# Two heads in turns on the two row halves of the array, in a three-layer mixer network on one core

## The chip, the cores and the metric

The kernel runs on 1 core of one Trainium2 chip. The metric is the time of one execution in device microseconds (us); shorter is better. Before the change the median of three runs is 2854.15 us (2843.81 to 2860.08).

## What is computed

One input of 512 tokens by 1024 features goes through a first block and two layers of a second block, all in float32. Cut to the parts that matter here:

```python
# first block: attention heads and a gated delta rule, 8 heads of 64 features, chunks of 64 tokens
a_mat = where(strict, (k_beta @ k.T) * decay, 0)           # per chunk, per head
qk    = where(causal, (q @ k.T) * decay, 0)
# after a triangular solve (u, w), chunk by chunk:
v_new = u - w @ state
o     = (q * exp(g)) @ state + qk @ v_new
state = state * exp(g_last) + k_dec.T @ v_new

# second block, each of two layers: three mixers a, b, c of 4 heads
#   a: heads of 128 features, c: heads of 64 features: a scan with decays by token, forward and backward
#   b: retention, heads of 64 features: scores (k.T q) * table of decays by distance, then times v
merged = sigmoid(gate_a) * (y_a @ w_pa) + sigmoid(gate_b) * (y_b @ w_pb) + sigmoid(gate_c) * (y_c @ w_pc)
x = x + g1 * (merged @ w_out)
# each block ends in a feed forward layer: (silu(h @ w_gate) * (h @ w_up)) @ w_down
```

## The kernel before, in words

Activations lie with features on the 128 partitions and the 512 tokens free. A large product (`proj`, L125) streams a strip of 128 weight columns from memory (`strip`, L104), splits it into two float32r parts on ScalarE and VectorE (`split`, L100), and sums three matmuls for each of up to 8 tiles of the contraction (`mm3`, L119 to L123: high by high, high by low, low by high). These products fill most of TensorE's time and are independent of one another within a stage.

PSUM is used through two tags of one bank a tile: `mm` with three buffers for the large products, `mx` with five for all else (L85 to L89). A buffer of `mx` is given out again only after what was in it has been read by VectorE or ScalarE.

Work is written as chains (delta rule, attention, scans, retention) into which a list of large products (`Dense`, L38) is mixed: `fill(us)` takes products worth about so many microseconds, by fixed costs. A framework then schedules the instructions of each engine by priority and its own cost model; on each engine they run in the order so found, and semaphores make them wait for their operands and buffers.

Many products contract over only 64 partitions, because two heads of 64 features share a tile: head e lies on partitions 64 e to 64 e + 63. Such a product uses one half of the array's rows. They are:

- `delta_pairs(h)` (L722): for each of 8 heads, four products k by k (L733) and four q by k (L734) of 64 rows, 128 columns, 128 tokens, into two tiles `mx`.
- `delta_out(t)` (L860): for each of 4 pairs of heads one tile `mx`. For each head and each tile of 128 tokens, a product of the masked scores (L870, 128 rows, 64 columns: the head's half of the columns), then one or two products with the state (L874, 64 rows and 64 columns: the head's quarter).
- `scan` (L1067): ten levels; s is 0 (the diagonal), then 1, 2, 4 to 256. At each level the two halves of every block of 2 s tokens meet. Mixer c calls it with two heads of 64 rows, mixer a with one head of 128. Up to s = 16 a level is 16 products per head of 32 columns (L1104); s = 32 and 64 go to L1123 (32 and 64 columns), s = 128 to L1135, s = 256 to `mm3` on the tiles `far`. Between levels VectorE multiplies the decays into `R` (L1154) and, up to s = 16, ScalarE copies the keys into `kt` (L1085); scores are written out into S by `split`.
- `retention(h)` (L1303): for each of 4 heads four tiles of scores, each one `mm3` over 64 rows (tile `bqk`, 512 tokens), then a product with the table of decays (L1315) and a `split` into `Sb`.

All four take one head after the other. In the scan, at s = 32 and 64, the loop over blocks b (which choose the columns of the array) is outside the loop over the tiles j of tokens, also in mixer a. In the second block retention of head h + 1 stands between the two halves of the work on head h (`mid`, a merge of 36 matmuls, L1433 to L1440).

Of the kernel before, what the change touches and what calls it, by code (L numbers as in the profile page):

```python
# [34 lines left out]
class Dense:  # L35
# [34 lines left out]
class Net:  # L70
# [78 lines left out]
    def first_pair(self):  # L149
        """the strips read at the start, behind the products that the next tiles of the operand wait for"""  # L150
# [8 lines left out]
    def go_on(self, last):  # L159
        """the next stage of the norm under way, its products after the one given"""  # L160
# [4 lines left out]
    def last_pair(self, ws, act, kn, then, norm):  # L165
        """two strips, one half of the tokens after the other; then(i, ps, sl) takes each, norm(sl) follows a half"""
# [16 lines left out]
    def proj_tok(self, w, act, dst):  # L183
        """tokens on partitions, 256 features free; dst(tt) takes tokens tt and tt + 1"""
# [68 lines left out]
    def setup2(self):  # L253
# [9 lines left out]
        # lower bounds of the second layer's forget gates  # L263
# [19 lines left out]
    def ada(self, li, g, part):  # L283
        """columns 512 g and on of layer li's modulation, a part of the rows"""
# [32 lines left out]
    def ada_sum(self):  # L317
        """a group's sum over the partitions, traced late so that it waits for nothing"""
# [15 lines left out]
    def ada_rows(self, li, g0, g1):  # L334
        """columns g0*1024 .. g1*1024, from rows to features on partitions"""
# [20 lines left out]
    def ada_first(self):  # L356
        """shift and gain of the first norm, some feature tiles at a time"""
# [67 lines left out]
    def stat(self, f, gained=False, sl=slice(0, T)):  # L425
        """running sums of squares, after x's tile f is final"""
# [11 lines left out]
    def rstd(self, hi, lo):  # L438
        """from squares over a head's partitions; 1 / 128 is exact"""
# [9 lines left out]
    # the norm's factors: a column for each tile of 128 tokens  # L449
# [21 lines left out]
    def spread(self, c):  # L471
        """columns to rows, on all partitions"""
# [1133 lines left out]
```

## Time and profile before

| | |
|---|---|
| runs | 2843.81, 2854.15, 2860.08 us, median 2854.15 |
| span of the profiled execution | 2841.0 us, granted TensorE clock 0.994 of full speed |
| TensorE (PE) busy | 2774.7 us, 98% |
| TensorE weight loads (PEld) busy | 2234.6 us, 79% |
| VectorE (DVE) busy | 1721.8 us, 61% |
| ScalarE (ACT) busy | 1172.0 us, 41% |
| DMA | 330.66 MB, mean 116 GB/s |

No time is given for the profiled execution apart from its span, so the span is taken as its own time; the fastest run is 2.8 us longer, the median 13.2 us.

How to read it: a matmul of this trace overlaps the next, so a row's time or an instruction's mean is longer than what it adds to the engine's time; the start of one row to the start of the next row is what the first one costs. A product in float32 stands in the trace as two matmuls (the program's one L870 is x2), one in float32r as one. The shapes read rows*columns of the array, then partitions x elements of the moving operand: `64*128 64x512` is 64 contracted rows, 128 columns, 512 tokens.

### The profile page before, as it was taken

What the parts mean: (1) busy time and instruction counts of PE and PEld (TensorE: products, weight loads), DVE (VectorE), ACT (ScalarE), POOL (GpSimd) and SP (SyncE); (2) the same over time, 40 slices, a digit from 0 to 9 for tenths busy, and PEclk for the clock granted to TensorE, in tenths of its full rate; (3) what the DMA queues carried; (4) which work ended last, traced back from release to release, by engine and by line L of the source; (5) the groups of instructions that cost most, each with busy time, mean ns of one, the idle gap of its engine ahead of it and who ended that gap; (6) DMA issues with size and microseconds to landing.
All of it is one profiled execution on the core that took longest, in us unless ns stands there. A gap on an engine that the chain in (4) does not pass through costs nothing.

```text
span 2841.0 us, 42612 instructions
## 1 busy us (share of the span) xinstructions
PE 2774.7 (98%) x17518; PEld 2234.6 (79%) x17518; DVE 1721.8 (61%) x2690; ACT 1172.0 (41%) x1796; POOL 41.7 (1%) x79
## 2 busy tenths in 40 slices
PE   7999999999999999999999999999999999999998
PEld 4786678878888887787887888877877888888887
DVE  4677646747377767756466563567777665533334
ACT  4643324222255655444343222465454443422223
POOL 0011000000000000100000000000000000000000
PEclk9999999999999999999999999999999999999999
DMA  7454524646232222332446463322223324333332
GB/s 259 126 157 117 156 87 144 228 150 215 84 110 62 68 72 68 101 93 83 133 134 210 153 224 93 103 66 68 68 75 90 99 80 130 89 97 96 92 94 82
DMA packets 471315, 330.66 MB, mean 116 GB/s; under 512 B 15447, under 2 KB 426223, under 8 KB 469584
## 3 DMA queue, kind: packets, MB, share of 16 engines
q1 hardware_dynamic: 468176, 320.51, 37.2%
q0 software_dynamic: 2944, 7.43, 0.9%
q8 instruction: 138, 2.26, 0.3%
q14 instruction: 57, 0.47, 0.1%
HBM read 312.55 MB, written 13.24 MB: 115 GB/s over the span
## 4 chain that ended last, share of the span: by engine, by line
PE 89%; DVE 4%; ACT 3%; DMA 2%; issue 1%; SPq 1%; POOL 0%; ACTq 0%; DVEq 0%; POOLq 0%
PE mm L121 22%; PE mm L122 22%; PE mm L123 22%; PE mx L121 3%; PE mx L122 3%; PE mx L123 3%; PE mm L193 1%; PE mm L195 1%; PE mm L194 1%; PE mx L1104 1%; PE mx L1123 1%; ACT whi L101 1%; PE mx L325 1%; PE mx L940 1%; DVE R L1154 1%
## 5 line engine op out<-in xcount | busy, mean ns | idle before, releaser
L121 PE MATMUL mm<-hh,whi 128*128 128x512 f32 (+1 forms) x2248 | 873.0, 391 | 12.4 <-ACT hh L487 9.0
L122 PE MATMUL mm<-hl,whi 128*128 128x512 f32 (+1 forms) x2248 | 876.9, 391 | 2.5 <-DVE hl L488 1.8
L101 ACT CAST whi<-raw 128x1024 fp32r<-128x1024 f32 (+2 forms) x451 | 438.3, 973 | 1068.6 <-PE mm L122 737.9
L123 PE MATMUL mm<-hh,wlo 128*128 128x512 f32 (+1 forms) x2248 | 874.0, 390 | 0.0
L102 DVE TENSOR_TENSOR wlo<-raw,whi 128x1024 fp32r<-128x1024 f32 (+2 forms) x451 | 507.4, 1126 | 361.5 <-ACT whi L101 350.0
L121 PEld LDWEIGHTS mm<-hh,whi 128*128 128x128 f32 x2248 | 419.6, 188 | 113.6 <-ACT hh L487 12.0
L122 PEld LDWEIGHTS mm<-hl,whi 128*128 128x128 f32 x2248 | 422.6, 188 | 102.5 <-DVE hl L488 6.0
L123 PEld LDWEIGHTS mm<-hh,wlo 128*128 128x128 f32 x2248 | 422.5, 188 | 93.4 <-issue 0.8
L122 PE MATMUL mm<-hid,whi 128*128 128x512 f32 (+1 forms) x564 | 212.7, 377 | 0.0
L121 PE MATMUL mm<-hid,whi 128*128 128x512 f32 (+1 forms) x564 | 212.5, 377 | 0.0
L123 PE MATMUL mm<-hid,wlo 128*128 128x512 f32 (+1 forms) x564 | 212.1, 376 | 0.0
L492 DVE SCALAR_TENSOR_TENSOR x<-mm,mod,x 128x512 f32<-128x512 f32 (+1 forms) x116 | 80.4, 694 | 180.6 <-PE mm L123 180.3
L307 DVE SCALAR_TENSOR_TENSOR acc<-araw,cs,acc 128x512 f32<-128x512 f32 x224 | 167.9, 750 | 17.6 <-DMA araw<-in_w_ada_dram 12.9
L542 DVE TENSOR_TENSOR sg<-mm,sg 128x512 f32<-128x512 f32 x66 | 45.6, 691 | 159.5 <-PE mm L123 158.0
L1154 DVE TENSOR_TENSOR R<-R,tot 128x512 f32<-128x512 f32 x192 | 126.0, 685 | 12.5 <-PE mx L1123 10.9
L193 PE MATMUL mm<-whi,hh 128*128 128x256 f32 x448 | 128.7, 287 | 2.0 <-ACT q_all L663 2.0
L195 PE MATMUL mm<-whi,hl 128*128 128x256 f32 x448 | 128.3, 286 | 0.0
L194 PE MATMUL mm<-wlo,hh 128*128 128x256 f32 x448 | 127.7, 285 | 0.0
L121 PEld LDWEIGHTS mm<-hid,whi 128*128 128x128 f32 x564 | 106.2, 188 | 20.4 <-issue 0.8
L122 PEld LDWEIGHTS mm<-hid,whi 128*128 128x128 f32 x564 | 106.2, 188 | 19.2
L123 PEld LDWEIGHTS mm<-hid,wlo 128*128 128x128 f32 x564 | 106.2, 188 | 19.1
L193 PEld LDWEIGHTS mm<-whi,hh 128*128 128x128 f32 x448 | 85.2, 190 | 4.3 <-ACT q_all L663 2.5
(384 smaller groups left out, 3507.2 us busy)
## 6 DMA issues: line engine op xcount, KB each, us to landing
raw<-in_w_in_dram SPq DMA_DIRECT2D x164, 512.0 KB
araw<-in_w_ada_dram SPq DMA_DIRECT2D x48, 1024.0 KB
raw<-in_w_ffn_in_dram SPq DMA_DIRECT2D x88, 512.0 KB
araw<-in_w_ada_dram SPq DMA_DIRECT2D x64, 256.0 KB
raw<-in_w_ffn_out_dram SPq DMA_DIRECT2D x32, 512.0 KB
raw<-in_w_gate_dram SPq DMA_DIRECT2D x22, 512.0 KB
raw<-in_w_up_dram SPq DMA_DIRECT2D x22, 512.0 KB
raw<-in_w_ada_dram SPq DMA_DIRECT2D x16, 512.0 KB
```

What stands on the lines that cost most here:

```text
L101: self.nc.scalar.copy(out=hi, in_=src)
L102: self.nc.vector.tensor_tensor(out=lo, in0=src, in1=hi.bitcast(F32), op=ALU.subtract)
L121: m(out=ps, lhsT=w[0], rhs=a[0], start=first, stop=False)
L122: m(out=ps, lhsT=w[0], rhs=a[1], start=False, stop=False)
L123: return m(out=ps, lhsT=w[1], rhs=a[0], start=False, stop=last)
L193: m(out=o, lhsT=a[0][:, sl], rhs=hi[:, k % 4], start=k == 0, stop=False)
L194: m(out=o, lhsT=a[0][:, sl], rhs=lo[:, k % 4], start=False, stop=False)
L195: m(out=o, lhsT=a[1][:, sl], rhs=hi[:, k % 4], start=False, stop=k == KT - 1)
L307: nc.vector.scalar_tensor_tensor(out=acc, in0=raw, scalar=cs[:, k:k + 1], in1=acc, op0=ALU.mult, op1=ALU.add)
L492: self.nc.vector.scalar_tensor_tensor(out=self.x(f)[:, sl], in0=ps[:, sl], scalar=g[:, f:f + 1], in1=self.x(f)[:, sl], op0=ALU.mult, op1=A ...
L542: nc.vector.tensor_tensor(out=sg, in0=pu, in1=sg, op=ALU.mult)
L1154: v.tensor_tensor(out=o, in0=o, in1=half(1 - c), op=ALU.mult)
```

## The change

The heads of a pair are taken in turns, so that matmuls that follow each other lie on different row halves: `delta_pairs` and `retention` work on a pair of heads at once, `scan` has its loop over heads innermost (and j outside b at s = 32 and 64), and `mm3s` interleaves the three matmuls of several products. `delta_out` first makes all products with the masked scores, the heads in turns, then all those with the state. All instructions other than matmuls stay the same in kind and number, but for three more loads of ScalarE's tables. `retention` now makes both heads' scores before the first `mid` of the pair. Comments are dropped throughout, so line numbers differ.

```diff
+    def mm3s(self, sets, first, last):
+        for i, (x, y) in enumerate(((0, 0), (0, 1), (1, 0))):
+            for ps, w, a in sets:
+                self.nc.tensor.matmul(out=ps, lhsT=w[x], rhs=a[y], start=first and i == 0, stop=last and i == 2)
...
-        def delta_pairs(h):
-            t, e = h // 2, h % 2
-            r = slice(64 * e, 64 * e + 64)
...
-            pk, pq = self.mx(), self.mx()
-            for tt in range(4):
-                sl = slice(tt * P, tt * P + P)
-                nc.tensor.matmul(out=pk[:, sl], lhsT=k_all[r, t, sl], rhs=k_all[r, t, sl], start=True, stop=True)
-                nc.tensor.matmul(out=pq[:, sl], lhsT=k_all[r, t, sl], rhs=q_all[r, t, sl], start=True, stop=True)
+        def delta_pairs(t):
+            gbs, rows = [], [slice(64 * e, 64 * e + 64) for e in range(2)]
...
+            ps = []
+            for x in (k_all, q_all):
+                ps.append([self.mx() for _ in rows])
+                for tt in range(4):
+                    sl = slice(tt * P, tt * P + P)
+                    for e, r in enumerate(rows):
+                        nc.tensor.matmul(out=ps[-1][e][:, sl], lhsT=k_all[r, t, sl], rhs=x[r, t, sl], start=True, stop=True)
...
-            for e in range(2):
-                h, o = 2 * t + e, slice(64 * e, 64 * e + 64)
-                wv = rv[h // 4]
-                for tt in range(4):
-                    sl = slice(tt * P, tt * P + P)
-                    nc.tensor.matmul(out=ps[o, sl], lhsT=wv[:, tt, h % 4, 0:64], rhs=qkm[h // 4][:, h % 4, sl],
-                                     start=True, stop=False)
-                    for c in range(max(1, 2 * tt), 2 * tt + 2):
-                        sl = slice(64 * c, 64 * c + 64)
-                        nc.tensor.matmul(out=ps[o, sl], lhsT=S[o, c, 64 * t:64 * t + 64], rhs=q_all[o, t, sl],
-                                         start=False, stop=c % 2 == 1)
+            hs = [(2 * t + e, slice(64 * e, 64 * e + 64)) for e in range(2)]
+            for tt in range(4):
+                sl = slice(tt * P, tt * P + P)
+                for h, o in hs:
+                    nc.tensor.matmul(out=ps[o, sl], lhsT=rv[h // 4][:, tt, h % 4, 0:64], rhs=qkm[h // 4][:, h % 4, sl],
+                                     start=tt == 0, stop=False)
+            for c in range(1, 8):
+                sl = slice(64 * c, 64 * c + 64)
+                for h, o in hs:
+                    nc.tensor.matmul(out=ps[o, sl], lhsT=S[o, c, 64 * t:64 * t + 64], rhs=q_all[o, t, sl],
+                                     start=False, stop=c == 7)
...
-                    for b in range(P // s):
-                        o, i = slice(s * b, s * b + s), s * (b ^ 1)
-                        for j in range(4):
-                            nc.tensor.matmul(out=ps4[o, j, i:i + s], lhsT=R[r, 1 + b % 2, j * P + s * b:j * P + s * b + s],
+                for j in range(4):
+                    for b in range(P // s):
+                        o, i = slice(s * b, s * b + s), s * (b ^ 1)
+                        for n, r in heads:
+                            m(out=four(near[n])[o, j, i:i + s], lhsT=R[r, 1 + b % 2, j * P + s * b:j * P + s * b + s],
...
-                            self.mm3(ps[:, j * 256:(j + 1) * 256], [a[r, o:o + P] for a in far[0]],
-                                     [a[r, 256 * (1 - b):256 * (2 - b)] for a in far[1]], True, True)
+                        self.mm3s([(ps[n][:, j * 256:(j + 1) * 256], [a[r, o:o + P] for a in far[0]],
+                                    [a[r, 256 * (1 - b):256 * (2 - b)] for a in far[1]]) for n, r in heads], True, True)
...
-        def retention(h):
+        def retention(t):
...
+            S = [[self.t8("Sb", F32R) for _ in range(2)] for _ in range(2)]
+            rows = [slice(64 * e, 64 * e + 64) for e in range(2)]
             for j in range(4):
-                ps = self.mx()
-                self.mm3(ps, [a[r, j * P:(j + 1) * P] for a in st["bk", t]], [a[r] for a in st["bq", t]], True, True)
...
+                ps = [self.mx() for _ in rows]
+                self.mm3s([(ps[e], [a[r, j * P:(j + 1) * P] for a in st["bk", t]], [a[r] for a in st["bq", t]])
+                           for e, r in enumerate(rows)], True, True)
...
-        S = retention(0)
-        for h in range(4):
-            mid(2 * h)
-            o = self.head_out(self.mix(st["bv"], h, S), V[:, 68 + h:69 + h], st["bg", h], y["b"], h)
-            next(o)
-            if h < 3:
-                S = retention(h + 1)
-            mid(2 * h + 1)
-            next(o)
+        for t in range(2):
+            S = retention(t)
+            for e in range(2):
+                h = 2 * t + e
+                mid(2 * h)
+                o = self.head_out(self.mix(st["bv"], h, S[e]), V[:, 68 + h:69 + h], st["bg", h], y["b"], h)
+                next(o)
+                mid(2 * h + 1)
+                next(o)
```

What the change does to TensorE's order, at two places. The first is the delta output, TensorE, before: the first head of a pair (`mx` the output tile, `qkm` and `rr` scores and values, `q_all` and `S` queries and state).

```order
L870 MATMUL mx<-qkm,rr 64x128
L874 MATMUL mx<-q_all,S 64x64
L870 MATMUL mx<-qkm,rr 64x128
L874 MATMUL mx<-q_all,S 64x64 x2
L870 MATMUL mx<-qkm,rr 64x128
L874 MATMUL mx<-q_all,S 64x64 x2
```

The kinds alternate at every token tile, eight times for a pair of heads. The same place now, two pairs of heads, down to the first large product:

```order
L882 MATMUL mx<-qkm,rr 64x128 x8
L887 MATMUL mx<-q_all,S 64x64 x14
L882 MATMUL mx<-qkm,rr 64x128 x8
L887 MATMUL mx<-q_all,S 64x64 x14
L683 MATMUL mx<-consts,osq 128x2 x4
L123 MATMUL mm<-ya,wlo 128x512
```

Each kind now stands in one row per pair of heads, and the work behind it is in the same order as before.

The second place is retention in the first layer of the second block, TensorE, before: head 0, the first of four tiles `mx` being number 10833 (10245 and 10246 are the high and low parts of queries and keys).

```order
L121 MATMUL mx_10833<-bqk_10245 128x512
L122 MATMUL mx_10833<-bqk_10246,bqk_10245 128x512
L123 MATMUL mx_10833<-bqk_10245,bqk_10246 128x512
L121 MATMUL mx_10841<-bqk_10245 128x512
L122 MATMUL mx_10841<-bqk_10246,bqk_10245 128x512
L123 MATMUL mx_10841<-bqk_10245,bqk_10246 128x512
```

After twelve of these a large product follows, and head 1 comes only after that and the product with v. Now, the first pair of heads (10835 is head 0, 10836 head 1):

```order
L129 MATMUL mx_10835<-bqk_10245 128x512
L129 MATMUL mx_10836<-bqk_10245 128x512
L129 MATMUL mx_10835<-bqk_10246,bqk_10245 128x512
L129 MATMUL mx_10836<-bqk_10246,bqk_10245 128x512
L129 MATMUL mx_10835<-bqk_10245,bqk_10246 128x512
L129 MATMUL mx_10836<-bqk_10245,bqk_10246 128x512
L129 MATMUL mx_10851<-bqk_10245 128x512
L129 MATMUL mx_10852<-bqk_10245 128x512
```

Twenty-four stand in a row, heads in turns. The second pair of heads now, from its second tile of scores on (11197 is head 2, 11198 head 3):

```order
L129 MATMUL mx_11197<-bqk_10245 128x512
L129 MATMUL mx_11197<-bqk_10246,bqk_10245 128x512
L129 MATMUL mx_11197<-bqk_10245,bqk_10246 128x512
L121 MATMUL mm_11251<-hh_6430,whi_11246 128x512
L122 MATMUL mm_11251<-hl_6431,whi_11246 128x512
L129 MATMUL mx_11198<-bqk_10245 128x512
L129 MATMUL mx_11198<-bqk_10246,bqk_10245 128x512
L129 MATMUL mx_11198<-bqk_10245,bqk_10246 128x512
```

Here the scheduler takes the heads one after the other again: of this pair only the six matmuls of the first tile are in turns. The second layer has the same order.

## Rows read from the trace of the kernel before

**Rows 1.** The page: TensorE's busy time, and the chain that ended last by engine.
```profile
PE 2774.7 (98%) x17518; PEld 2234.6 (79%) x17518; DVE 1721.8 (61%) x2690; ACT 1172.0 (41%) x1796; POOL 41.7 (1%) x79
...
PE 89%; DVE 4%; ACT 3%; DMA 2%; issue 1%; SPq 1%; POOL 0%; ACTq 0%; DVEq 0%; POOLq 0%
```

**Rows 2.** Busy time by stage, scans of c: length; busy PE, PEld, DVE, ACT, POOL.
```profile
855.00:970.00 115.00, 111.38 (x1401) 90.76 (x1400) 89.98 (x167) 69.06 (x119) 0.00 (x0) 1.00 0.24 66
```

**Rows 3.** Timeline of TensorE, one pair of heads in delta output: start us, us, instructions.
```profile
394.47 1.09 PE L686 MATMUL mx<-c_ident,hc 128*64 128x128 f32 x16 [0.95 <-DVE hc L460]
395.39 0.38 PE L870 MATMUL mx<-qkm,rr 128*64 128x128 f32 x2
...
400.98 0.83 PE L677 MATMUL mx<-consts,osq 128*128 128x2 f32 x6
```

**Rows 4.** Timeline of TensorE, one step of the delta states.
```profile
359.88 0.68 PE L846 MATMUL mx<-S,m 64*64 64x64 f32 x16
360.50 0.50 PE L121 MATMUL mm<-ya,whi 128*128 128x512 f32 x1
```

**Rows 5.** Timeline of TensorE, delta pairs of heads 0 and 1.
```profile
91.85 0.48 PE L733 MATMUL mx<-k_all 64*128 64x128 f32 x2
...
93.30 0.49 PE L733 MATMUL mx<-k_all 64*128 64x128 f32 x4
93.52 0.49 PE L734 MATMUL mx<-q_all,k_all 64*128 64x128 f32 x4
93.85 0.38 PE L733 MATMUL mx<-k_all 64*128 64x128 f32 x2
...
95.28 0.50 PE L121 MATMUL mm<-hh,whi 128*128 128x512 f32 x1
```

**Rows 6.** Timeline of TensorE, one scan of mixer c: s = 1, 32, 64, 128, 256.
```profile
861.36 0.84 PE L1104 MATMUL mx<-R,kt 64*32 64x32 f32 x64 [2.73 <-ACT kt L1085]
...
882.21 1.51 PE L1123 MATMUL mx<-R 64*32 64x32 f32 x64 [0.52 <-DVE R L1154]
...
885.48 1.54 PE L1123 MATMUL mx<-R 64*64 64x64 f32 x32
...
888.78 1.71 PE L1135 MATMUL mx<-R 64*128 64x128 f32 x16
...
897.14 0.51 PE L121 MATMUL mx<-far 64*128 64x256 f32 x4
...
900.22 0.50 PE L121 MATMUL mx<-S,cvh 128*128 128x512 f32 x1
```

**Rows 7.** Groups by line, 338.2 to 340.4 us, delta transitions: busy us, mean ns.
```profile
L819 PE MATMUL mx<-kdec,rr 64*64 64x64 f32 x64 | 2.1, 225 | 0.0
L820 PE MATMUL mx<-qkm,rr 64*64 64x64 f32 x64 | 2.1, 218 | 0.0
```

**Rows 8.** Timeline of TensorE, one scan of mixer a: s = 1, 32, 64.
```profile
988.04 0.55 PE L1104 MATMUL mx<-R,kt 128*32 128x32 f32 x32
...
1005.86 0.90 PE L1123 MATMUL mx<-R 128*32 128x32 f32 x32
...
1008.31 0.97 PE L1123 MATMUL mx<-R 128*64 128x64 f32 x16
```

**Rows 9.** Timeline of TensorE, retention of head 0, start and end.
```profile
1242.38 0.49 PE L121 MATMUL mx<-bqk 64*128 64x512 f32 x1
1242.72 0.39 PE L122 MATMUL mx<-bqk 64*128 64x512 f32 x1
1242.96 0.39 PE L123 MATMUL mx<-bqk 64*128 64x512 f32 x1
...
1245.35 0.50 PE L121 MATMUL mm<-hh,whi 128*128 128x512 f32 x1
```

**Rows 10.** Busy time by stage: scan of c between s = 64 and 256; behind retention.
```profile
887.10:897.10 10.00, 10.00 (x51) 7.79 (x51) 9.01 (x21) 7.25 (x19) 0.00 (x0) 1.00 0.19 54
1243.40:1249.40 6.00, 6.00 (x26) 4.61 (x25) 6.00 (x9) 2.84 (x5) 0.00 (x0) 1.00 0.36 90
```

More of the change, by code (lines that the diff above doesn't have):

```diff
@@ new lines, in delta_pairs @@
+        def delta_pairs(t):
+            gbs, rows = [], [slice(64 * e, 64 * e + 64) for e in range(2)]
+            for e in range(2):
+                h = 2 * t + e
+                gb = self.t2("gb")
+                nc.sync.dma_start(out=gb, in_=bass.AP(gs.tensor, gs.offset + h * T, [[0, P], [1, T]]))
+                v.tensor_tensor(out=four(gb), in0=four(gb), in1=cap(rt, 16 + h, [[32, 4], [0, P]]), op=ALU.subtract)
+                v.scalar_tensor_tensor(out=four(gb), in0=four(gb), scalar=0.0, in1=mask(dmask), op0=ALU.min, op1=ALU.add)
+                nc.scalar.activation(out=gb, in_=gb, func=AF.Exp)
+                gbs.append(gb)
+            ps = []
[5 more added lines that the diff above has]
+                        nc.tensor.matmul(out=ps[-1][e][:, sl], lhsT=k_all[r, t, sl], rhs=x[r, t, sl], start=True, stop=True)
+            for e in range(2):
+                h = 2 * t + e
+                nt = self.t2("nt")
+                v.tensor_tensor(out=nt, in0=ps[0][e], in1=gbs[e], op=ALU.mult)
+                nc.gpsimd.dma_start(out=nts[4 * h:4 * h + 4].rearrange("t (j i) -> j t i", j=P), in_=four(nt))
+                last = v.tensor_tensor(out=four(noff[h // 4][:, h % 4]), in0=four(nt), in1=mask(off), op=ALU.mult)
+                v.tensor_tensor(out=qkm[h // 4][:, h % 4], in0=ps[1][e], in1=gbs[e], op=ALU.mult)
+            if t == 1:
@@ L975, in mixer1 @@
             delta_tok(t)
-            for e in range(2):
-                delta_pairs(2 * t + e)
+            delta_pairs(t)
             q_decay(t)
@@ L1091, in scan @@
                 yield
-            for n, r in heads:
-                if s <= 16:
-                    if lv % 4 == 0:
+            m = nc.tensor.matmul
+            if s <= 16:
+                if lv % 4 == 0:
+                    for n, r in heads:
                         small[n] = self.mx()
-                    ps = small[n][:, (lv % 4) * P:(lv % 4) * P + P]
-                    for j in range(4):
-                        for b in range(4):
-                            o = j * P + 32 * b
+                pss = {n: small[n][:, (lv % 4) * P:(lv % 4) * P + P] for n, r in heads}
+                for j in range(4):
+                    for b in range(4):
+                        o = j * P + 32 * b
+                        for n, r in heads:
                             if s == 0:
@@ L1115, in scan @@
                             put(n, o, 32 * b, [[T + P, 4], [1, 32]], four(sd[n][o]))
-                elif s <= 64:
-                    if s == 32:
+            elif s <= 64:
+                if s == 32:
+                    for n, r in heads:
                         near[n] = self.mx()
-                    ps4 = four(near[n])
+                for j in range(4):
                     for b in range(P // s):
                         o, i = slice(s * b, s * b + s), s * (b ^ 1)
-                        for j in range(4):
-                            nc.tensor.matmul(out=ps4[o, j, i:i + s], lhsT=R[r, 1 + b % 2, j * P + s * b:j * P + s * b + s],
-                                             rhs=R[r, 3 - 3 * (b % 2), j * P + i:j * P + i + s], start=True, stop=True,
-                                             tile_position=(r.start, s * b))
-                    if s == 64:
+                        for n, r in heads:
+                            m(out=four(near[n])[o, j, i:i + s], lhsT=R[r, 1 + b % 2, j * P + s * b:j * P + s * b + s],
+                              rhs=R[r, 3 - 3 * (b % 2), j * P + i:j * P + i + s], start=True, stop=True,
+                              tile_position=(r.start, s * b))
+                if s == 64:
+                    for n, r in heads:
                         for s2 in (32, 64):
```

71 lines of the change are left out of this document (31 added, 40 removed).

## The prediction

> **What bounds the kernel now.** I read the page's busy times and its chain first, then the busy times by stage, then TensorE's timeline at each of the products that the change touches, and last what VectorE does there.
>
> TensorE is busy 2774.7 us of a span of 2841.0, and 89% of the chain that ended last lies on it [rows 1]. So a matmul that takes less of the array's time shortens the end, provided that the next thing on TensorE is ready. The second half of this sentence is open only in the scans and retention: in the first scans of mixer c TensorE is busy 111.4 of 115 us, but VectorE 90.0 [rows 2], and single levels already start late, by 0.52 us behind VectorE and 2.73 us behind ScalarE [rows 6]. In the delta rule the products stand in queues of large products that need nothing of them.
>
> **How products on parts of the array run, by rows.** Three places in this trace show it. First, column halves: the products L686 (64 columns, halves in turns) take 0.92 us for 16 records from their start to the next row's start [rows 3]. Second, quarters: in the delta states L846 the even head is on rows and columns 0 to 63, the odd one on 64 to 127, in turns and into one tile; 16 records take 0.62 us [rows 4]. And in the delta transitions, where all four quarters come in turns, 128 records of the same size take 2.1 us, 16 ns each [rows 7]. Third, row halves with all 128 columns, which is what most of the change needs: there is no such sequence, but one seam. In delta pairs 32 records take 3.43 us from 91.85 to 95.28, so four take 0.43. At the step from head 0 to head 1, eight records take only 0.55 us, from 93.30 to 93.85, instead of 0.86 [rows 5]. The last product of one head and the first of the next lie on different halves there, so they overlap: the eight cost 0.64 of their serial time. As a seam has a serial product at each side, I take this as the upper bound of a pair's price and 0.5 as the lower one, and work with 0.55.
>
> **The sum, part by part** (a row's start to the next row's start is its cost; where rows of one kind are compared, their own lengths do).
>
> *Delta output*, four pairs of heads. One pair costs 400.98 - 395.39 = 5.59 us [rows 3]: 16 records of L870 and 28 of L874 that change kind sixteen times. Grouped, the 16 records are of L686's shape, in column halves in turns: 0.92 us [rows 3]. The 28 are of L846's: 28/16 of 0.62 = 1.09 us [rows 4]. The sum is 2.0, the gain 3.6 a pair, **14.3 us**. What follows on TensorE, the norm's sums over the pair before, is one round behind and stays covered by the next pair's 2.0 us.
>
> The two heads' state products here write one tile from two row halves. The Trainium skill (TensorEngine Tiling (Array Packing), Restrictions and Gotchas, Gotcha 1) says that different row tiles cannot access the same PSUM bank at the same time. The states L846 do just that and reach 39 ns a record, where 64 by 64 products that mostly stay in one quarter need (1.54 us for 32) 48 [rows 4, 6], so the trace speaks against the rule; by the rule the 28 records would cost 1.35 us instead of 1.09, and the sum would be 1 us smaller.
>
> *Delta pairs*, four: 3.43 us each [rows 5] become 0.55 of that, 1.89: **6.2 us** (4.9 to 6.9 by the two prices). The group now holds four tiles `mx` of five at once instead of two and two; the two transposes ahead of it occupy two, whose last reader is done before the second pair of tiles is asked for, so I charge nothing but cover it with 0.8 us below.
>
> *Scans of c*, four (two layers, two pairs of heads) [rows 6]. s = 32: 64 records in 1.51 us; the same number and size at s = 1, where the column groups come in turns, takes 0.84: 0.67. s = 64: 1.54 us become the transitions' 32 x 16 ns = 0.5 plus a tail of 0.2: 0.84 [rows 6, 7]. s = 128: 1.71 us at 0.55 to 0.6 with the tail: 0.7. s = 256: from 897.14 to 900.22 are 3.08 us with one large product of about 0.25 inside; 0.45 of the other 2.83 goes: 1.27 (1.0 to 1.4). The sum is 3.48 a scan, **13.9 us**. Levels up to s = 16 already cost some 13 ns a record with four column groups; eight tiles instead of four may give up to 0.1 us a level. I count nothing.
>
> *Scans of a*, eight [rows 8]: here only b and j change places, so that column groups come in turns. s = 32: 0.90 becomes the 0.55 of s = 1: 0.35. s = 64: 0.97 becomes the 0.68 of L846, two halves in turns [rows 4]: 0.29. **5.1 us**.
>
> *Retention*, four heads in each of two layers. Twelve products cost 2.97 us from 1242.38 to 1245.35 [rows 9]. The first pair of heads, 5.94, becomes 24 products in turns, at 0.55 3.27 us. But now eight tiles of scores pass through five buffers: VectorE gives a buffer back after an instruction of 0.67 us (nine instructions in the 6.00 us behind the group, without a pause [rows 10]), and its splits stand in between. The sixth to eighth tile wait for the first three, about 0.8 us. That leaves 1.9. Of the second pair of heads the scheduler keeps six products in turns and takes the rest apart: 0.65 gained, and 0.1 lost for each time that TensorE changes between these and large products more often than before (1242.72 - 1242.38 is 0.34, the next step 0.24 [rows 9]): 0.5. **4.8 us** for both layers (2 to 7).
>
> The parts add up to 14.3 + 6.2 + 13.9 + 5.1 + 4.8 = **44.3 us**.
>
> *What comes back.* Between s = 64 and 256 in the scan shown, VectorE is busy 9.0 of 10.0 us, TensorE all of it with large products [rows 10]. The work of VectorE there (decays, 14 pieces of scores to split, a strip) doesn't shrink, and only its start moves. Of the 1.5 us saved at s = 64 and 128 I let 1.2 come back as a wait at s = 256, in one of two scans a layer (the other has more large products in that place): 2.4. In the scans of a 1.2 for all eight, in delta pairs 0.8. Edits without cost: the nt product ahead of qkm in delta pairs moves no work, three more table loads lie on ScalarE, at 41% [rows 1], behind large products. 44.3 - 4.4 = 39.9 us. Against the profiled execution that is 2841.0 to 2801.1, and with the same difference the median of 2854.15, which lies 13.2 above that span, becomes **2814 us**.
>
> **Rivals.**
>
> *Evictions decide in the second block.* If in the scans and in retention VectorE and ScalarE are always the later ones, TensorE's gain there (13.9 + 5.1 + 4.8) returns as waits, and only the delta rule's 19.7 us stay: 2834. For it speaks VectorE at 78% [rows 2] and the levels that start late [rows 6]; against it, that a level's products are part of the chain themselves: VectorE can't update R before they end, so it starts earlier too. The Trainium skill (TensorEngine Tiling (Array Packing), Performance Considerations, PSUM Bottleneck) warns of this: tiling speeds up TensorE, not the reading of PSUM. Chance 0.16.
>
> *Row halves with 128 columns don't run side by side.* Then delta pairs, s = 128, s = 256 and retention (6.2 + 2.8 + 5.1 + 4.8) gain nothing, and some 24 us are left: 2830. The seam speaks against it [rows 5]. Chance 0.07.
>
> *Slower: TensorE stands at full buffers.* It takes its instructions in order, and both heads' tiles are now filled before either is read. If every eviction had to be waited for, retention would hold TensorE for eight times two instructions of 0.67 us, 10.7 less its own 3.3, four times: 30 us; s = 128 and 256, with eight such instructions beyond their products, four times 5: 21; delta pairs, six evictions of 0.67 less 1.9, four times: 8. That is 59 against 44.3, some 15 us slower: 2869. It decides only if over three quarters of these evictions are uncovered. Against it: behind each group stand large products that need no `mx` tile. Chance 0.03.
>
> *The change doesn't do what it says*: the scheduler separates the heads, as it does in half of retention, or what is gained is lost in the placing of large products. About 2852, chance 0.05.
>
> **How the numbers follow.** The forecast has 0.69. A measurement of this kernel can tell about 0.5% from no change, 14.3 us: faster by more than that is below 2839.9. The forecast and nearly all of the first two rivals lie there: 0.88; the same 0.09; slower 0.03. The range: at the low end all bounds at their best and nothing coming back (44.3 + 6, so 2804) and runs that differ by 16 us among themselves, 2797; at the high end both rivals around 2830 to 2834, 2837.
>
> **What would show it.** Right: the rows of delta output at about 2 us a pair; eight records of delta pairs in some 0.47 us; TensorE's busy time about 44 us lower at the same count of records; its waits at `R`, `kt` and `far` up by less than 6 us. Wrong: matmuls of different halves that start one after the other; TensorE waiting at L129 for the products with the table; VectorE without pauses through whole scans while TensorE waits.

## The result and the profile after

The changed kernel takes 2814.27 us (median of 4 runs, 2812.23 to 2818.36) against 2854.11 us of the kernel before in the same series: ratio 0.987, 95% interval 0.985 to 0.989. A second series gave 2816.97 against 2850.55, ratio 0.988 (0.986 to 0.990). It is 1.3% faster, with an interval that lies clear of 1, and where the prediction put it. The page of the profiled execution, span 2810.5 us:

```profile
PE 2743.8 (98%) x17518; PEld 2203.2 (78%) x17518; DVE 1718.7 (61%) x2690; ACT 1173.7 (42%) x1799; POOL 41.7 (1%) x79
```

The count of matmuls is the same, TensorE's busy time is 30.9 us lower [rows 1], the span is 30.5 us shorter. The forecast said 44 and 40; where the difference lies is the question of the runs below. First the places that the prediction named.

TensorE's timeline (start us, us, instructions, idle time before), one pair of heads in delta output: 1.94 us from 382.45 to 384.39, instead of 5.59 [rows 3]; 2.0 was forecast.

```profile
382.45 1.04 PE L882 MATMUL mx<-qkm,rr 128*64 128x128 f32 x16
383.43 1.03 PE L887 MATMUL mx<-q_all,S 64*64 64x64 f32 x28
384.39 1.05 PE L683 MATMUL mx<-consts,osq 128*128 128x2 f32 x8
```

Delta pairs of heads 0 and 1 are 2.28 us, from 88.78 to 91.06, instead of 3.43 [rows 5]. The forecast was 1.89. The second pair of heads, from 111.89, needs only 1.99 us.

```profile
88.78 1.16 PE L744 MATMUL mx<-k_all 64*128 64x128 f32 x16
...
91.06 0.50 PE L121 MATMUL mm<-hh,whi 128*128 128x512 f32 x1
...
111.89 1.16 PE L744 MATMUL mx<-k_all 64*128 64x128 f32 x16
...
113.88 0.50 PE L121 MATMUL mm<-hh,whi 128*128 128x512 f32 x1
```

The difference is a buffer. In the first group the fourth tile must wait until VectorE has read the transposes of v, and that instruction runs into the group:

```profile
89.18 0.68 DVE L726 TENSOR_TENSOR rr<-mx,rt 128x512 f32<-128x512 f32 x1
```

The first products of head 1 with q start 0.23 us behind those of head 0, and the group is 0.29 us longer for it. The third group has the same wait (2.16 us), the fourth doesn't (1.99).

The first scan of c, by the rows' lengths: s = 32 is 0.76 us (1.51 before), s = 64 0.69 (1.54), s = 128 1.16 (1.71) [rows 6]. At s = 256, by starts and with the large product that stands inside, it is 2.43 us from 876.54 to 878.97 instead of 3.08.

```profile
863.57 0.76 PE L1139 MATMUL mx<-R 64*32 64x32 f32 x64 [0.64 <-DVE R L1174]
...
866.08 0.69 PE L1139 MATMUL mx<-R 64*64 64x64 f32 x32
...
868.72 1.16 PE L1153 MATMUL mx<-R 64*128 64x128 f32 x16
...
876.54 0.50 PE L129 MATMUL mx<-far 64*128 64x256 f32 x4
876.97 0.50 PE L121 MATMUL mm<-hh,whi 128*128 128x512 f32 x1
...
878.97 0.49 PE L121 MATMUL mx<-S,cvh 128*128 128x512 f32 x1
```

At s = 256 the gain is 0.65 us in this scan, where 1.27 was forecast. The kernel before shows why:

```profile
897.58 0.50 PE L121 MATMUL mm<-hh,whi 128*128 128x512 f32 x1
898.01 0.38 PE L122 MATMUL mx<-far 64*128 64x256 f32 x1
...
898.83 0.28 PE L123 MATMUL mx<-far 64*128 64x256 f32 x1
898.83 0.38 PE L122 MATMUL mx<-far 64*128 64x256 f32 x1
```

The large product inside costs 0.43 us from its start to the next, not the 0.25 of the prediction, so the other 24 cost 2.65. And these 24 were not all one after the other: the first four, two of each head, take 0.44 us from 897.14 [rows 6], as the four do that are now in turns (0.43), and where head 1 follows head 0 the last products of one and the first of the other start together (898.83). Some ten of the 24 already ran in pairs.

Behind the scan stand the products with its scores S, TensorE, and VectorE's part of writing S out of the tiles `mx`, the changed kernel and then the kernel before:

```profile
879.69 0.50 PE L122 MATMUL mx<-S,cvh 128*128 128x512 f32 x1 [0.23 <-DVE S L102]
...
878.95 1.89 DVE L102 TENSOR_TENSOR S<-mx,S 128x512 fp32r<-128x512 f32 x3 [1.57 <-ACT S L101]
```

```profile
899.52 2.48 DVE L102 TENSOR_TENSOR S<-mx,S 128x512 fp32r<-128x512 f32 x4 [1.86 <-ACT S L101]
```

Before, head 0's tiles were complete while head 1's were still being made, and VectorE began 0.70 us before the first product with S (900.22). Now both heads' tiles end together and it begins as that product starts (878.97), so TensorE has to wait for the scores.

A scan of a: s = 32 takes 0.46 us instead of 0.90, s = 64 0.69 instead of 0.97 [rows 8].

```profile
983.60 0.46 PE L1139 MATMUL mx<-R 128*32 128x32 f32 x32
...
985.60 0.69 PE L1139 MATMUL mx<-R 128*64 128x64 f32 x16
```

Retention, first pair of heads, TensorE and then VectorE: 4.91 us from 1217.32 to 1222.23 instead of twice 2.97 [rows 9].

```profile
1217.32 1.89 PE L129 MATMUL mx<-bqk 64*128 64x512 f32 x13
1220.14 2.16 PE L129 MATMUL mx<-bqk 64*128 64x512 f32 x11 [0.94 <-DVE s L1335]
1222.23 0.50 PE L121 MATMUL mm<-hh,whi 128*128 128x512 f32 x1
```

```profile
1218.27 1.23 DVE L102 TENSOR_TENSOR wlo<-raw,whi 128x1024 fp32r<-128x1024 f32 x1 [5.30 <-ACT whi L101]
1219.41 1.88 DVE L1335 TENSOR_TENSOR s<-mx,tab 128x512 f32<-128x512 f32 x3
```

Thirteen products complete four tiles and begin the fifth. VectorE turns to a strip's split of 1.23 us just when the first tiles are complete, so the first buffer comes back only after 1219.41. TensorE waits 0.94 us and then works off the other eleven as buffers come, in 2.09 us, where six pairs at the 0.23 of a large product would be 1.4.

### The profile page after: what moved, and what is told of

It reads as the page before. It is cut to its first block, busy times and chain, and to the rows that moved or that the text cites. A ratio compares the mean times of both kernels' runs of the same rounds, so it can differ in the third digit from the quotient of the medians.

```text
span 2810.5 us, 42619 instructions
## 1 busy us (share of the span) xinstructions
PE 2743.8 (98%) x17518; PEld 2203.2 (78%) x17518; DVE 1718.7 (61%) x2690; ACT 1173.7 (42%) x1799; POOL 41.7 (1%) x79
## 3 DMA queue, kind: packets, MB, share of 16 engines
q1 hardware_dynamic: 468176, 320.51, 37.6%
## 4 chain that ended last, share of the span: by engine, by line
PE 85%; DVE 5%; ACT 4%; DMA 2%; issue 2%; SPq 1%; POOL 0%; DVEq 0%; ACTq 0%; POOLq 0%
PE mm L121 22%; PE mm L122 22%; PE mm L123 22%; PE mx L122 2%; PE mx L121 2%; PE mx L123 2%; PE mm L199 1%; PE mm L201 1%; PE mm L200 1%; ACT whi L101 1%; PE mx L1118 1%; PE mx L129 1%; DMA araw<-in_w_ada_dram 1%; DVE R L1174 1%; DVE wlo L102 1%
## 5 line engine op out<-in xcount | busy, mean ns | idle before, releaser
L452 DVE RECIPROCAL rstd<-rstd 128x512 f32<-128x512 f32 x24 | 80.4, 3351 | 13.4 <-ACT rstd L451 13.4
```

The costliest lines, as they stand in the source:

```text
L452: nc.vector.reciprocal(out=r, in_=r)
```

## The experiments

Single runs of one kernel differ by up to 23 us, as much as a term of the sum. Most of that goes with TensorE's clock (below): over the 83 runs whose clock is on record, 41 of them of the kernel before, I fitted one time for each kernel and one slope for the run's mean granted clock. The slope is -2.07 us for 0.001 of clock, and what is left scatters by 1.75 us. Differences "at equal clock" are from this fit, with two standard errors. The runs come from several chips; an offset of its own for each chip moves no difference between kernels with several runs by more than 0.5 us.

### Each part undone

Four kernels are the changed one with one function of before put back:

```diff
+            for n, r in heads:
...
-                for j in range(4):
                     for b in range(P // s):
                         o, i = slice(s * b, s * b + s), s * (b ^ 1)
-                        for n, r in heads:
...
+                        for j in range(4):
...
```

> The changed kernel with the scan of before; all else as changed. Theory of the sum (TensorE's time in the scans is on the path): the scans' terms 13.9 + 5.1 come back, less the 3.6 that I let them lose to waits, so 15.4 us over the changed kernel's 2814, some 2829, ratio to before 0.991. Rival (VectorE and ScalarE decide in the scans, what TensorE saves there returns as waits): within 3 us of the changed kernel, 2814 to 2817, ratio 0.987. Third, on the clock: the changed kernel's profiled execution had a mean granted clock of 0.990 and that of before 0.994. If the small products in turns bring the clock down, this kernel's clock rises to 0.992 or more in its runs; if it is a matter of the single execution, it scatters as that of the others does.

Measured: 2828.26 us (2824.95 to 2834.12), ratio 0.993 (0.991 to 0.994). At equal clock it is 12.4 ± 1.9 us slower than the changed kernel. The rival falls: TensorE's time in the scans is on the path. The mean clock of its runs, 0.988 to 0.991, did not rise.

```diff
-            for tt in range(4):
-                sl = slice(tt * P, tt * P + P)
-                for h, o in hs:
...
+            for e in range(2):
+                h, o = 2 * t + e, slice(64 * e, 64 * e + 64)
+                wv = rv[h // 4]
+                for tt in range(4):
...
```

> The changed kernel with the delta output of before. Theory of the sum: 14.3 us over the changed kernel, 2828, ratio to before 0.991; a pair of heads takes 5.6 us again on TensorE. Rival (the norm's sums of the pair before were what the pairs waited for, so a shorter pair only waits longer): 2814 to 2818.

Measured: 2831.12 us (2827.63 to 2836.44), ratio 0.993 (0.992 to 0.995); 13.4 ± 1.9 us at equal clock. The rival falls; the term is there in full.

```diff
-                self.mm3s([(ps[e], [a[r, j * P:(j + 1) * P] for a in st["bk", t]], [a[r] for a in st["bq", t]])
-                           for e, r in enumerate(rows)], True, True)
+                self.mm3(ps, [a[r, j * P:(j + 1) * P] for a in st["bk", t]], [a[r] for a in st["bq", t]], True, True)
...
+            if h < 3:
+                S = retention(h + 1)
```

> The changed kernel with the retention of before, one head after the other. Theory of the sum: 4.8 us over the changed kernel, 2819. By the changed kernel's trace, where the first pair of heads waits 0.94 us for a buffer in each layer and the products in turns are broken up, it is about 3 us: 2817. Rival (the wait at the full buffers and the later scores cost more than the turns gain): 2810 to 2813.

Measured: 2819.82 us (2814.84 to 2820.40), ratio 0.989 (0.987 to 0.991); 2.7 ± 2.1 us at equal clock: nearer to the 3 that the trace of the changed kernel says than to the forecast's 4.8, which lies at the edge of the interval. The rival falls.

```diff
-            delta_pairs(t)
+            for e in range(2):
+                delta_pairs(2 * t + e)
```

> The changed kernel with the delta pairs of before, one head after the other. Theory of the sum: 6.2 less the 0.8 kept back, 5.4 us over the changed kernel, 2819; in the trace 32 records take 3.43 us again instead of 2.1 to 2.3. Rival (TensorE has pauses in this stage anyway, behind the squares of the norm, and a shorter group only waits longer there): 2814 to 2816, the pauses of TensorE between 90 and 175 us shorter than the changed kernel's.

Measured: 2820.36 us (2819.50 to 2821.98), ratio 0.989 (0.987 to 0.991); 4.2 ± 2.0 us at equal clock. The group is 3.43 us again, from 91.90 to 95.33 in its timeline. By the rival TensorE's pauses between 90 and 175 us would be shorter here than in the changed kernel; the view of waits has 3.0 us there, and 1.9 and 2.6 in the changed kernel's two executions. They are not shorter, so the rival falls, and the time is longer by the term within the error.

The four parts add up to 32.7 us, the whole change to 33.6 ± 1.4 at equal clock: within the errors the parts do not get in each other's way.

| part | forecast, net of waits | TensorE's time saved, by the traces | new waits there | by the runs |
|---|---|---|---|---|
| delta output | 14.3 | 14.5 | 0 | 13.4 |
| delta pairs | 5.4 | 5.3 | 0 | 4.2 |
| scans, c and a | 15.4 | 17.5 | 5.8 | 12.4 |
| retention | 4.8 | 5.5 | 2.3 | 2.7 |
| all | 39.9 | 42.8 | 8.1 | 33.6 |

The third column compares the second profiled executions of both kernels: for each matmul its end less the end of the one before, pauses left out, summed over the rows of a kind. The waits of retention, and 3.0 us of those of the scans, are from the view of waits there (engine, line, waited for: us in total, times, longest). Changed kernel, span 2814.2:

```profile
PE mx L129 <- ACT far L101: 3.5, 7, 1.0
PE mx L1139 <- DVE R L1174: 2.4, 4, 0.7
PE mx L129 <- DVE s L1335: 1.9, 2, 0.9
PE mx L122 <- DVE S L102: 0.9, 4, 0.2
PE mx L129 <- DVE far L102: 0.9, 1, 0.9
PE mx L1153 <- DVE R L1174: 0.6, 2, 0.3
PE mx L129 <- ACT rstd L451: 0.4, 2, 0.2
```

The kernel before, span 2844.9:

```profile
PE mx L1123 <- DVE R L1154: 2.0, 3, 0.9
PE mx L121 <- ACT far L101: 1.8, 6, 0.4
PE mx L122 <- DVE far L102: 0.6, 1, 0.6
```

At `far` 2.4 became 4.4, at `R` 2.0 became 3.0, and 2.3 us at retention's buffers and behind them are new: 5.3 us. The wait for `kt`, 6.7 us, is the same in these two. Another 2.8 us stand at the first products with the scores of mixer c's scans (`mx<-S,cvh`), as shown above. By the third column's measure these products take 16.7 us instead of 15.2, and the pauses before them, of which the view has 0.9 at `S`, are 1.2 us where there were none. Both figures are the same in both executions of either kernel, and with the scan of before put back both are gone again (15.2 and none). 42.8 less 8.1 is 34.7 us, and the runs give 33.6 ± 1.4.

### The clock

> The kernel before, once more, for the granted clock of its runs. In the one profiled execution that the prediction is made against it was 0.994, in the four runs of the changed kernel 0.989 to 0.991. Theory (the clock falls after pauses of TensorE by the chance of the single execution, with either kernel): the clocks of this kernel's runs scatter, their mean is 0.989 to 0.992, and the longer runs are those with the lower clock. Rival (the products in turns bring the clock down): this kernel stays at 0.993 to 0.995 and the change has a hidden cost of some 9 us.

> The changed kernel once more, on the same chip as the kernel before and the spread retention, for its clock and as what the spread retention is compared with: 2814, ratio to before 0.987, clocks 0.989 to 0.991. If chance rules the clock, one or two runs at 0.992 or more; if the change lowers it, none.

The kernel before ran in 2843.51 to 2853.59 us (median 2847.77) at mean clocks of 0.988 to 0.991; its other 29 runs in these series lie between 0.983 (2864.86 us) and 0.993 (2842.08 us). The changed kernel: 2816.97 us (2815.37 to 2819.51), 0.988 to 0.990. The means over all these runs, 41 and 8, are 0.9893 and 0.9898. So the change does not lower the clock. One sign that was named came out against this: none of the changed kernel's eight runs has 0.992 or more. But only two of the 41 of the kernel before have it, so the sign was a weak one. The one profiled execution of the kernel before, at 0.994, was an unusually good one; none of the 41 runs reached that. Its busy time lacks what a lower clock added to the others, which is why TensorE's busy time seemed to fall by only 30.9 us. Between the second executions (0.991 and 0.990) it falls from 2780.3 to 2742.7, by 37.6.

Busy time by stretch (length; busy PE, PEld, DVE, ACT, POOL; granted clock, DMA) shows how it comes. The kernel before, second execution:

```profile
820.00:824.00 4.00, 2.75 (x15) 2.47 (x15) 3.89 (x10) 2.31 (x6) 0.00 (x0) 0.82 0.78 240
824.00:828.00 4.00, 4.00 (x28) 4.00 (x28) 3.18 (x9) 1.92 (x5) 0.00 (x0) 0.76 0.00 0
1864.00:1868.00 4.00, 0.16 (x2) 0.00 (x0) 1.79 (x2) 3.97 (x4) 0.00 (x0) 0.88 0.00 0
1868.00:1872.00 4.00, 2.37 (x70) 2.31 (x71) 4.00 (x9) 1.57 (x3) 0.00 (x0) 0.50 0.02 4
```

The same kernel, first execution, the second of these stretches:

```profile
824.00:828.00 4.00, 4.00 (x34) 3.83 (x33) 3.66 (x12) 2.44 (x7) 0.00 (x0) 1.00 0.00 0
```

At 1864 TensorE stands still for nearly 4 us and then runs at 0.50, the lower of its two levels (1.2 of 2.4 GHz). From 820 to 824 it is busy for 2.75 of 4 us in both executions; in the second the clock is lower after the pause (0.82, 0.76), and from 824 to 828 there pass 28 matmuls where 34 did in the first, whose clock stays at 1.00. So much the same pause was followed by a lower clock in one execution and not in the other, and a single execution can be lucky at several such places.

### Delta output taken apart

Kinds in a row, but one head after the other:

```diff
-            for tt in range(4):
-                sl = slice(tt * P, tt * P + P)
-                for h, o in hs:
+            for h, o in hs:
+                for tt in range(4):
+                    sl = slice(tt * P, tt * P + P)
...
-            for c in range(1, 8):
-                sl = slice(64 * c, 64 * c + 64)
-                for h, o in hs:
+                for c in range(1, 8):
+                    sl = slice(64 * c, 64 * c + 64)
```

> The changed kernel's delta output with each kind of product in a row per head, but one head after the other. Theory (the old 5.59 us were two things: 16 + 28 records one after the other, some 16 x 0.111 + 28 x 0.048 = 3.1 us, and 15 changes of kind at 0.16 us, 2.5 us; turns halve the first, grouping removes the second): 3.1 us and three changes, about 3.4 us a pair of heads, against the changed kernel's 1.94. Rival 1 (the changes of kind were all, turns bring nothing): 1.9 to 2.1. Rival 2 (turns are all, a change of kind costs nothing): over 5.

Heads in turns, but the kinds alternating from tile to tile of tokens:

```diff
             for tt in range(4):
                 for h, o in hs:
...
-            for c in range(1, 8):
-                sl = slice(64 * c, 64 * c + 64)
-                for h, o in hs:
+                for c in range(max(1, 2 * tt), 2 * tt + 2):
+                    sl = slice(64 * c, 64 * c + 64)
+                    for h, o in hs:
```

> The changed kernel's delta output with the heads in turns, but the kinds alternating from one tile of 128 tokens to the next, as before. Theory: 1.94 us of products in turns and six more changes of kind at 0.16 us, about 3.0 us a pair of heads. Rival 1 (the changes of kind were all): over 3.5. Rival 2 (a change of kind costs nothing): 1.9 to 2.1.

Timelines of a pair of heads, first the kinds in a row:

```profile
376.64 1.09 PE L882 MATMUL mx<-qkm,rr 128*64 128x128 f32 x8
377.66 1.02 PE L886 MATMUL mx<-q_all,S 64*64 64x64 f32 x14
...
380.59 1.09 PE L882 MATMUL mx<-qkm,rr 128*64 128x128 f32 x8
```

and the heads in turns:

```profile
381.82 0.44 PE L882 MATMUL mx<-qkm,rr 128*64 128x128 f32 x4
382.19 0.33 PE L887 MATMUL mx<-q_all,S 64*64 64x64 f32 x4
...
384.70 0.44 PE L882 MATMUL mx<-qkm,rr 128*64 128x128 f32 x4
```

Without turns a pair is 3.95 us (3.4 was expected), without grouping 2.88 (3.0); with neither it was 5.59, and the changed kernel has 1.94. Both rivals of either run fall. Six more changes of kind cost (2.88 - 1.94) / 6 = 0.16 us each, as expected. The turns are worth more than expected: one head alone takes 1.02 and 0.96 us for half the products, as long as both heads together in the changed kernel. Here the second head is free. Four pairs at 2.0 and 0.9 us more are 8.0 and 3.8 us; the single times, 2825.55 and 2823.80 us, are 5.9 and 2.1 us over the changed kernel at equal clock, each ± 3.8, and don't contradict that.

One tile for each head:

```diff
-            ps = self.mx()
+            pt = [self.mx() for _ in range(2)]
...
-                    nc.tensor.matmul(out=ps[o, sl], ...
+                    nc.tensor.matmul(out=pt[o.start // 64][o, sl], ...
```

> The changed kernel's delta output with one tile mx for each head, so that the two row halves never write the same PSUM bank; VectorE and ScalarE read the two tiles by halves. Theory (one tile costs nothing): the 28 products with the state take 0.96 us as in the changed kernel. Rival, by the rows of the scan of before, where 64 by 64 products in one quarter take 0.048 us and a pair on two quarters might take that for both: 28 x 0.024, 0.7 us. The Trainium skill (TensorEngine Tiling (Array Packing), Restrictions and Gotchas, Gotcha 1) says that different row tiles cannot access one PSUM bank at the same time, which would make this kernel the faster one.

```profile
394.30 1.03 PE L887 MATMUL mx<-q_all,S 64*64 64x64 f32 x28
```

The 28 products take 0.96 us (394.30 to the next row at 395.26), as in one tile. Two row halves that write one tile lose nothing here, where they write different partitions of it; two that write the same partitions of one tile stand in no run. By the rule of the Trainium skill (TensorEngine Tiling (Array Packing), Restrictions and Gotchas, Gotcha 1), as the expectation reads it, the kernel with two tiles should have been the faster; the trace doesn't bear that out. The single time, 2816.27 us, is 2.9 ± 3.7 us over the changed kernel at equal clock, so it shows no gain either.

### Turns of column groups, or of heads

```diff
-                for j in range(4):
-                    for b in range(P // s):
-                        o, i = slice(s * b, s * b + s), s * (b ^ 1)
-                        for n, r in heads:
+                for n, r in heads:
+                    for j in range(4):
+                        for b in range(P // s):
+                            o, i = slice(s * b, s * b + s), s * (b ^ 1)
```

and the same at every other level, with `mm3` for each head in place of `mm3s`; both heads' tiles are still asked for first.

> The changed kernel's scan with tiles of tokens outside column groups at s = 32 and 64, but one head after the other at every level. Theory (column groups in turns are enough at s = 32; the heads in turns matter where a head has one or two column groups): in the scans of c s = 32 takes 0.8 us as in the changed kernel, s = 64 1.2 us instead of 0.69 (twice the 0.61 of a head of mixer a), s = 128 1.64 instead of 1.16, s = 256 2.8 instead of 2.0; the scans of a as changed. Rival (row halves in turns do all of it): s = 32 stays at 1.5 as before the change.

```profile
867.50 0.76 PE L1139 MATMUL mx<-R 64*32 64x32 f32 x64 [0.53 <-DVE R L1175]
...
870.00 0.97 PE L1139 MATMUL mx<-R 64*64 64x64 f32 x32
...
872.73 1.71 PE L1153 MATMUL mx<-R 64*128 64x128 f32 x16
...
881.96 0.39 PE L122 MATMUL mx<-far 64*128 64x256 f32 x2
882.18 0.28 PE L123 MATMUL mx<-far 64*128 64x256 f32 x2
```

At s = 32 the column groups do everything: 0.76 us, as with both kinds of turns. At s = 64 it is 0.97 against 0.69 (1.2 was expected), at s = 128 1.71 against 1.16 (1.64). At s = 256 the expectation is wrong: the products start two at a time, 0.12 us apart, and take what they take in the changed kernel. TensorE's order there, with the tiles' numbers (7323 is one head, 7324 the other):

```
L122 MATMUL mx_7323<-far_7318,far_7315 128x256
L123 MATMUL mx_7323<-far_7317,far_7316 128x256
L122 MATMUL mx_7324<-far_7318,far_7315 128x256
L123 MATMUL mx_7324<-far_7317,far_7316 128x256
L121 MATMUL mx_7323<-far_7317,far_7315 128x256
```

The heads do not alternate one by one: two or three products of one head come first, then as many of the other. Still both rows of a line start together, so a product of the second head does not wait behind those of the first. The single time, 2817.03 us, can't be told from the changed kernel's at equal clock (-0.5 ± 3.7 us).

### Retention spread out

```diff
-            return S
+                yield S
...
+        two = lambda t: [next(runs[t]) for _ in range(2)][0]
...
+        two(0)
+        mid(next(mids))
+        S = two(0)
+        mid(next(mids))
+        for h in range(4):
...
+            if h == 0:
+                two(1)
+            mid(next(mids))
+            next(o)
+            if h == 0:
+                S1 = two(1)
```

The eight merges `mid` are all there, some of them earlier.

> The changed kernel, but the four steps of a pair's scores come two at a time, with a merge of 36 large products between the twos. Theory (the buffers, not the turns, took the rest of retention's gain): no wait at the products with the table, 12 records in turns in about 1.6 us (six times 0.23 and the start), four of these a layer, 6.4 us a layer instead of the changed kernel's 10.0: 7 us faster, 2807, ratio 0.9845. Rival (VectorE decides in this stretch, so what TensorE gains it waits for at the next product with the scores): 2814, waits at the products with S or at the norm's sums up by 3 us a layer.

> The retention in twos with a merge between, once more, beside the changed kernel on one chip. By the trace of its first run (5 groups of 1.59 to 0.96 us a layer and no wait at the table, against 9.1 us and a wait of 0.94) it should be 5 to 6 us faster than the changed kernel, ratio to before 0.985. Rival (what it saves returns elsewhere): as the changed kernel, 0.987.

```profile
1221.66 1.66 PE L129 MATMUL mx<-bqk 64*128 64x512 f32 x12
1223.25 0.50 PE L121 MATMUL mm<-hh,whi 128*128 128x512 f32 x1
```

The first run gave 2810.25 us (2807.97 to 2816.24), ratio 0.986 (0.985 to 0.988), the second 2812.09 (2808.43 to 2814.20), 0.986 (0.984 to 0.988). By the ratios alone that can't be told from the changed kernel. At equal clock, over nine runs, it is 6.3 ± 1.7 us faster, and the trace says why: twelve products take 1.59 us, three times in each layer (the last twelve are split into nine and three, 1.59 and 0.89 us), the wait of 1.9 us at the table is gone, and no wait elsewhere has grown by that. By the rows, in each layer the first pair of heads takes 3.18 us instead of 4.91, which is the room for its tiles, and the second pair 4.07 instead of 5.15, as the scheduler now keeps more of it in turns; over both layers that is 5.6 us. It is the best version of this study: turns and room for the tiles belong together.

## Why the prediction was right, and where it was off

The time was right, 2814 against 2814.27, and the likeliest case was the one that came. The gain behind it was about 6 us too large: 39.9 us against 33.6 at equal clock. That the time came out to within 0.3 us all the same is luck: the 39.9 were taken from the median of the first three runs, 2854.15, while the 41 later runs of the kernel before have a mean of 2850.5; and of the changed kernel's two series the first was the lower one (2814.27 against 2816.97).

- *What bounds the kernel*: right. Undoing the parts one by one gives 32.7 of the 39.9 us back, and TensorE is as busy as before (98%). The first rival, that evictions decide in the second block, is refuted by the scan undone: 12.4 us. Its core holds for a part: 8.1 of 42.8 us returned as waits for VectorE and ScalarE, and 6 were forecast with retention's buffers. The Trainium skill (TensorEngine Tiling (Array Packing), Performance Considerations, PSUM Bottleneck) warns of this, and the traces agree for the 1.9 us at retention's tiles and the 2.8 us at the scores, where VectorE and ScalarE read `mx` tiles; the 3.0 us at `R` and `far` are waits for decays, which lie in no `mx` tile.
- *Row halves with 128 columns run side by side*: right, the second rival falls. The first thirteen products of retention take 1.89 us; in serial order twelve took 2.97 [rows 9].
- *The price of a pair, 0.55*: right for long groups, a little low for short ones. A group also has a start and an end at which nothing overlaps: 32 records of delta pairs without a wait come to 1.99 / 3.43 = 0.58 of their serial time, the 16 of s = 128 to 1.16 / 1.71 = 0.68. Delta pairs gave 5.3 us gross instead of 6.2, of which some 0.5 went into the waits for a buffer, for which 0.8 had been kept back. The scans of a gave 5.8 instead of 5.1.
- *s = 256*: the term of the sum that was mis-sized most. Its four groups gave 2.9 us by the third column's measure instead of 5.1, because the 2.83 us that were multiplied by 0.45 were 2.65, and ten of the 24 products already ran in pairs. This is nearly all that the scans of c lack, 11.7 us gross instead of 13.9.
- *Delta output*: right, 1.94 us against 2.0, and both of its reasons were shown: turns and changes of kind. One tile written from two row halves, each on its own partitions, costs nothing, as taken.
- *What comes back in the scans*: too little, and in other places. 3.6 us were forecast, 2.4 of them at `far` in one scan of c a layer and 1.2 in the scans of a; the traces have 5.8, at `far` and `R`, and 2.8 of it at the products with the scores of c, which the prediction doesn't name.
- *Retention*: off. The wait for a buffer was forecast at 0.8 and is 0.94 us, but then the rest was priced as if it ran on in turns. After the wait TensorE gets buffers one at a time, which costs another 0.7 us a layer. 4.8 became 2.7 by the runs, and spreading the tiles gives the loss back. The wait at L129 for the table, which the prediction names as a sign of being wrong, came here and nowhere else.
- *Slower, or nothing done*: neither. TensorE stood at full buffers for 1.9 us in retention and for some 0.5 in the delta pairs.
- *The signs*: eight records of delta pairs take 0.45 us in a group without a wait (0.47 was forecast), and the waits at `R`, `kt` and `far` rose by 3.0 us, less than the 6 named. TensorE's busy time fell by 37.6 us between the second executions, not by 44: for s = 256, retention and the products with the scores.

## What to carry to other kernels

Products that use half of the rows should come in turns with those of the other half, and in long groups of one kind, since each change of kind cost 0.16 us here and each group has a start and an end without overlap. Look first for places where the halves already meet, since products that run in pairs there gain nothing. Before putting more products side by side, count the tiles that they fill at once against the buffers, and put other work of the same engine between where they don't suffice; and note that heads in turns are also finished together, so the one that came first is read later. And price a change against more than one execution: here one good clock in the profiled run was worth as much as a term of the sum.

## What the runs showed that I had not expected

- Strict alternation isn't needed: with two or three products of one head ahead of as many of the other, the pairs still started together (s = 256 with heads apart, 0.12 us a pair). The second pair of heads in retention shows it too: three products of head 2 and then three of head 3 take 0.90 us:

```profile
1269.41 0.97 PE L129 MATMUL mx<-bqk 64*128 64x512 f32 x6
1270.31 0.50 PE L121 MATMUL mm<-hh,whi 128*128 128x512 f32 x1
```

With sixteen of a head in a row, as in the delta pairs of before, only some products at the seam did [rows 5].
- In delta output eight products of one head take the same 1.0 us as sixteen of two heads in turns.
- The runs of one kernel differ by up to 23 us, and by the fit 21 of them go with the mean granted clock, 0.983 to 0.993.
- With the heads of a scan in turns, the writing out of their scores begins later than with one head after the other, and TensorE lost 2.8 us by it over the four scans of c.
